# The state-space recurrence of a hybrid encoder on chunks of 8 steps instead of full-length scans

## The chip, the cores and the metric

One core of a Trainium2 chip runs the kernel. The metric is device time in microseconds (us) from the first to the last instruction of a run. The core has a matrix engine (TensorE, PE in the rows; its weight loads are PEld), a vector engine (VectorE, DVE), a scalar engine (ScalarE, ACT), a general engine (GpSimd, POOL) and a queue engine (SyncE, SP) that starts most transfers. Each engine takes its instructions in one fixed order and waits on semaphores for the others.

## What is computed

The reference is a trunk of two layers on 512 tokens of width 1024. Each layer has a mixer (three token mixers on the same input, gated and merged) and a mixture of 16 experts. The change touches the first token mixer, S5, a diagonal state-space model: 256 channels in 16 groups of 16, each group with 64 complex states. Cut to what matters, with the complex arithmetic as in the reference:

```python
lam_bar = jnp.exp(lam * dt)                       # (16 groups, 64 states), complex
b_bar = b * ((lam_bar - 1.0) / lam)[..., None]    # (16, 64, 16)
bu = einsum('blgc,gpc->blgp', uf, b_bar)          # input of every step
# state[t] = lam_bar * state[t-1] + bu[t], t = 0 .. 511
y = (einsum('blgp,gcp->blgc', real(states), c_re) - einsum('blgp,gcp->blgc', imag(states), c_im)
     + d_skip * uf)
y = gelu(y); y = y * sigmoid(y @ w_glu + b_glu)
```

The other two token mixers are stick-breaking attention (4 heads, a running sum along the keys) and chunkwise retention. Their sum, gated, goes through an output projection, a norm, the experts and another norm. All is held to single precision.

## The kernel before

**Matmuls and weights.** A large product in single precision is three passes with operands cut into a high and a low part (`mm3`, L343 to L345). A weight chunk comes by SyncE's queue (`load`, L317), ScalarE copies its high part `wh` (L337), and VectorE or GpSimd subtracts it from the raw values for the low part `wl` (L338), in halves of 128x1024. Which of the two engines does it in a mixer's chunk is a table, `LEND`. In the expert loops VectorE does nearly all of them.

**A layer.** The projection of the mixers runs in 22 chunks of 256 columns. Chunk 0 is the input of S5 (`s5_in`). Chunks 1 to 3 are queries, keys and values of the attention (`stick`): the first three chunks are made with tokens along the free axis (`pjf`, matmuls of 512 columns), the values with channels there (`pjt`, 256 columns). Ten units of attention follow, each a score product, two sigmoids on ScalarE, a scan on VectorE (L735), a product `take` (L737), transposes and a value product `pw` (L740 to L746). Then come retention (chunks 4 to 9), the gates (10 to 21), the output projection and the experts.

**S5 before.** `s5_params` makes, from the parameters, the table b (`bb`, split and spread into `small`), the decay `mag` and the table E of 128 powers of the unit rotation of each state, by doubling (L585 to L590). For layer 0 it runs on VectorE while the first chunks are projected, with half of the last doublings on GpSimd. For layer 1 it is a generator on GpSimd that takes a step in each expert loop of layer 0 from expert 4 on. `s5` then takes eight blocks of 128 states: six matmuls for real and imaginary inputs `bre` and `bim` over 512 tokens, six rotations by E (L642 to L647), two scans in four pieces of 128 with a carry fixed up between them (L658 to L662), six operations to rotate back (L664 to L669, one of them on GpSimd), and two fp32 matmuls `py` with the table c (L672, L673). Gelu and the gate `glu` (L689) end it.

**What sets the order.** A scheduler places the instructions of each engine in a fixed order, by the order of the program and by priorities. The parts of S5 are placed among the attention and the projections; `bre`, `bim` and `py` have high priority on TensorE.

Of the kernel before, what the change touches and what calls it, by code (L numbers as in the profile page):

```python
# [9 lines left out]
F32 = mybir.dt.float32  # L10
F32R = mybir.dt.float32r
# [8 lines left out]
P = 128  # L20
# [34 lines left out]
ST = SMALL["b"][0]  # L55


def shape_constants():
# [12 lines left out]
    misc[:, 40:48] = 2.0 ** np.arange(8)  # L71
# [20 lines left out]
def lay_out(a):  # L92
# [10 lines left out]
    for n in ("s5_d", "s5_b_glu", "ret_gn_g", "ln1_g", "ln1_b"):  # L103
# [3 lines left out]
    c = np.zeros((DEPTH, 2, 64, 2, 2, 4, 2, 16), np.float32)  # L107
    for ri, n in enumerate(("s5_c_re", "s5_c_im")):
        v = a[n].reshape(DEPTH, 2, 4, 2, 16, 64)
        for g in range(2):  # L110
            c[:, g, :, :, ri, :, g, :] = v[:, :, :, g].transpose(0, 4, 1, 2, 3)
    put("c", c)
# [4 lines left out]
    return dict(small=sm, router=rw)  # L117


class Kernel:  # L120
# [340 lines left out]
    def s5_loads(self, l, queue=None):  # L461
        self.s5b = self.sx[0].tile([P, ST + 2 * T], F32, tag="raw", name="small")
        sm = self.s5b[:, 0:SM]
        at = SMALL["c"][0]
        self.nc.scalar.dma_start(sm[:, 0:at], self.a["small"][l][:, 0:at])
        for i, j in ((ST, SM), (at, ST)):
            self.loaded = (queue or self.nc.scalar).dma_start(sm[:, i:j], self.a["small"][l][:, i:j]).ins
        return sm
# [5 lines left out]
    def s5_params(self, sp, sm, V, two):  # L474
        nc, mp = self.nc, self.keep
        bn = self.part(sm, "b").rearrange("p (r i c) -> p r i c", r=2, i=8)
        st2 = lambda nm, n, dt=F32, bufs=1: sp.tile([P, n], dt, tag=nm, name=nm, bufs=bufs)
        re, im, ldt = (self.part(sm, n) for n in ("s5_lambda_re", "s5_lambda_im", "s5_log_dt"))
        t = lambda nm, n=8: sp.tile([P, n], F32, name=nm, tag=nm)
        dt = self.poly_exp(sp, ldt, 8, V)  # L480
# [3 lines left out]
        mag = mp.tile([P, 8], F32, tag="mag", name="mag")  # L484
        V.tensor_copy(mag, self.poly_exp(sp, x, 8, V))
        N = 8 * LEVELS
        ang = sp.tile([P, LEVELS, 8], F32, name="ang")
        V.tensor_tensor(ang, th[:, None, :].to_broadcast([P, LEVELS, 8]),
                        self.misc[:, 40:40 + LEVELS, None].to_broadcast([P, LEVELS, 8]), OP.mult)
        af = ang.rearrange("p a b -> p (a b)")  # L490
# [25 lines left out]
        En = mp.tile([P, 2, LEVELS, 8], F32, tag="En", name="En")  # L516
        V.tensor_scalar(En[:, 0], cm.rearrange("p (a b) -> p a b", a=LEVELS), 1.0, None, OP.add)
        V.tensor_copy(En[:, 1], s.rearrange("p (a b) -> p a b", a=LEVELS))
        turn = mp.tile([P, 8, 2], F32, tag="turn", name="turn")
        V.tensor_copy(turn[:, :, 0], En[:, 1, 7])  # L520
        V.tensor_scalar(turn[:, :, 1], En[:, 1, 7], -1.0, None, OP.mult)
        lr, l1, li = t("lr"), t("l1"), t("li")
        V.tensor_tensor(lr, mag, cm[:, 0:8], OP.mult)
        V.tensor_tensor(lr, lr, mag, OP.add)
        V.tensor_scalar(l1, lr, -1.0, None, OP.add)
        V.tensor_tensor(li, mag, s[:, 0:8], OP.mult)
# [16 lines left out]
        v4 = lambda t, n=256: t[:, 0:n].rearrange("p (r i c) -> p r i c", r=2, i=8)  # L543
        zrb = zr[:, :, None].to_broadcast([P, 8, 16])
        zib = zi[:, :, None].to_broadcast([P, 8, 16])
        bb = v4(st2("bb", 256))
        q = st2("Et0", 256, bufs=2)[:, 0:128].rearrange("p (i c) -> p i c", i=8)
        V.tensor_tensor(bb[:, 0], bn[:, 0], zrb, OP.mult)
        V.tensor_tensor(q, bn[:, 1], zib, OP.mult)
        V.tensor_tensor(bb[:, 0], bb[:, 0], q, OP.subtract)  # L550
        V.tensor_tensor(bb[:, 1], bn[:, 0], zib, OP.mult)
        V.tensor_tensor(q, bn[:, 1], zrb, OP.mult)
        self.stt(V, bb[:, 1], bb[:, 1], -1.0, q, OP.mult, OP.subtract)
        bh = v4(st2("bh", 256, F32R))
        bl = bb
        yield
        nc.scalar.copy(bh, bb)
        yield
        V.tensor_tensor(bl, bb, bh.bitcast(F32), OP.subtract)
        for m in range(2):  # L560
            yield
            st = self.s5b[:, ST + m * T:ST + (m + 1) * T]
            sv = st.rearrange("p (k r q c) -> p k r q c", k=2, r=2, q=4)
            nc.gpsimd.memset(st, 0.0)
            for k, src in enumerate((bh.bitcast(F32), bl)):
                for g2 in range(2):
                    pp = slice(g2 * 64, g2 * 64 + 64)
                    V.tensor_copy(sv[pp, k, :, :, g2 * 16:g2 * 16 + 16], src[pp, :, 4 * m:4 * m + 4])
        yield
        e2 = self.sx[1].tile([P, 2 * 8 * P], F32, tag="raw", name="E")  # L570
        er, ei = (e2[:, i * 8 * P:(i + 1) * 8 * P].rearrange("p (a b) -> p a b", a=8) for i in range(2))
        nc.gpsimd.memset(er[:, :, 0:1], 1.0)
        nc.gpsimd.memset(ei[:, :, 0:1], 0.0)
        for j in range(LEVELS - 1):
            n = 2 ** j
            last = j >= LEVELS - (4 if two == 2 else 2)
            for hf, G in ((slice(0, 4), V), (slice(4, 8), nc.gpsimd)) if last else ((slice(0, 8), V),):
                w = hf.stop - hf.start
                cr = En[:, 0, j, hf, None].to_broadcast([P, w, n])
                ci = En[:, 1, j, hf, None].to_broadcast([P, w, n])  # L580
                a0, b0 = er[:, hf, 0:n], ei[:, hf, 0:n]
                a1, b1 = er[:, hf, n:2 * n], ei[:, hf, n:2 * n]
                t0 = st2(f"Et{hf.start * (two - 1)}", 256, bufs=2)[:, 0:w * n].rearrange("p (i n) -> p i n", i=w)
                t1 = st2(f"Et{hf.start * (two - 1)}", 256, bufs=2)[:, 0:w * n].rearrange("p (i n) -> p i n", i=w)
                G.tensor_tensor(a1, a0, cr, OP.mult)  # L585
                G.tensor_tensor(t0, b0, ci, OP.mult)
                G.tensor_tensor(b1, b0, cr, OP.mult)
                G.tensor_tensor(t1, a0, ci, OP.mult)
                G.tensor_tensor(a1, a1, t0, OP.subtract)
                G.tensor_tensor(b1, b1, t1, OP.add)  # L590
        E = [(er[:, 0:4], ei[:, 0:4]), (er[:, 4:8], ei[:, 4:8])]
        self.s5w = dict(mag=mag, En=En, turn=turn, E=E, sm=sm,
                        cT=self.part(sm, "c").rearrange("p (m r s) -> p m r s", m=2, r=2),
                        wg=self.part(sm, "w_glu").rearrange("p (k c) -> p k c", k=2))

    def s5_in(self, l, hh):
        nc = self.nc
        V = nc.vector
# [883 lines left out]
```

## Time and profile before

| what | value |
|---|---|
| three runs, median (lowest to highest) | 2286.53 us (2275.9 to 2291.71) |
| span of the profiled execution | 2285.9 us |
| time of that execution | 2285.9 us: nothing of note lies outside the span |
| TensorE busy | 2169.5 us |
| VectorE busy | 1738.9 us |
| ScalarE busy | 1228.1 us |
| GpSimd busy | 443.2 us |

Busy is the time in which an engine executes. The rest of the span it waits or issues. The share is an average over stages that differ: in the two mixers (about 20 to 300 us and 1157 to 1400 us) TensorE has gaps, in most of the expert loops it has none. The granted clock is the share of full speed (2.4 GHz) that TensorE gets; half of it is 1.2 GHz.

### The profile page before, as it was taken

Reading aid. Unit: us, or ns where it says so; the run is one execution under the profiler, and the core shown is the slowest. Engines: PE = TensorE matmul, PEld = TensorE weight load, DVE = VectorE, ACT = ScalarE, POOL = GpSimd, SP = SyncE. Lnnn points to the kernel's source line nnn. Section 1 sums busy time; section 2 is a strip of 40 time slices with the busy share of each in tenths; the row PEclk is TensorE's granted clock in tenths of the full one; section 3 lists DMA queues with packets and bytes.
Section 4 is the critical chain, followed back from the end, with each engine's and each line's share of the span. In section 5 each row is a group of like instructions: output and inputs, shape, how many; then the busy total and the mean of one; then the engine's idle time right before and its main releaser. Section 6 shows DMA issues by size and latency. Waiting matters only on the chain. (4 is left out here: it accounts for less than half of the span.)

```text
span 2285.9 us, 27438 instructions
## 1 busy us (share of the span) xinstructions
PE 2169.5 (95%) x10068; PEld 1586.7 (69%) x10069; DVE 1738.9 (76%) x2339; ACT 1228.1 (54%) x1526; POOL 443.2 (19%) x469
## 2 busy tenths in 40 slices
PE   6998999999999799999988989999899999999997
PEld 5656678877777577776655566888777777777765
DVE  8778753458988988887888875334689888888878
ACT  3231123336777577777732321232377777777774
POOL 4322051120049510000232210511300000000003
PEclk9898999999999899999999999999999999999999
DMA  5402245327989799997821021453289999999965
GB/s 184 152 32 57 65 152 187 113 79 286 339 313 350 266 360 345 338 376 278 344 92 56 19 70 65 166 180 120 79 318 336 358 345 359 349 351 359 345 256 212
DMA packets 180006, 517.22 MB, mean 226 GB/s; under 512 B 9808, under 2 KB 63696, under 8 KB 179856
## 3 DMA queue, kind: packets, MB, share of 16 engines
q1 hardware_dynamic: 167424, 475.91, 57.0%
q10 hardware_dynamic: 7312, 20.28, 2.5%
q0 software_dynamic: 5120, 19.14, 2.3%
q8 instruction: 82, 1.34, 0.2%
q14 instruction: 68, 0.56, 0.1%
HBM read 490.38 MB, written 22.81 MB: 225 GB/s over the span
## 5 line engine op out<-in xcount | busy, mean ns | idle before, releaser
L338 DVE TENSOR_TENSOR wl<-raw,wh 128x1024 fp32r<-128x1024 f32 x834 | 1025.3, 1247 | 275.3 <-ACT wh L337 258.1
L337 ACT CAST wh<-raw 128x1024 fp32r<-128x1024 f32 x872 | 906.1, 1050 | 489.2 <-PE e L345 210.7
L344 PE MATMUL e<-wl,hx 128*96 128x512 f32 x1024 | 406.6, 397 | 18.9 <-DVE wl L338 15.3
L345 PE MATMUL e<-wh,hx 128*96 128x512 f32 x1024 | 404.1, 395 | 0.0
L343 PE MATMUL e<-wh,hx 128*96 128x512 f32 x1024 | 391.9, 394 | 0.3 <-ACT wh L337 0.3
L344 PE MATMUL pjf<-hx,wh 128*128 128x512 f32 x608 | 246.3, 405 | 5.2 <-DVE hx L211 5.1
L343 PE MATMUL pjf<-hx,wh 128*128 128x512 f32 x608 | 247.7, 408 | 1.6 <-DVE v L210 1.6
L345 PE MATMUL pjf<-hx,wl 128*128 128x512 f32 x608 | 245.7, 404 | 0.0
L344 PEld LDWEIGHTS e<-wl,hx 128*96 128x96 f32 x1024 | 165.6, 162 | 87.2 <-DVE wl L338 14.1
L343 PEld LDWEIGHTS e<-wh,hx 128*96 128x96 f32 x1024 | 165.4, 162 | 67.7 <-ACT wh L337 0.7
L345 PEld LDWEIGHTS e<-wh,hx 128*96 128x96 f32 x1024 | 165.7, 162 | 65.6
L345 PE MATMUL e<-wh,gl 128*96 128x512 f32 x512 | 201.3, 393 | 0.0
L344 PE MATMUL e<-wl,gh 128*96 128x512 f32 x512 | 201.1, 393 | 0.2
L343 PE MATMUL e<-wh,gh 128*96 128x512 f32 x512 | 194.7, 393 | 0.0
L1335 POOL DMA_INDIRECT yg<-yd,pos x16 | 27.4, 1714 | 856.0 <-DMA raw<-in_moe_w_dram 843.1
L344 PEld LDWEIGHTS pjf<-hx,wh 128*128 128x128 f32 x608 | 117.1, 193 | 40.9 <-issue 9.4
L343 PEld LDWEIGHTS pjf<-hx,wh 128*128 128x128 f32 x608 | 117.1, 193 | 33.6 <-issue 7.6
L345 PEld LDWEIGHTS pjf<-hx,wl 128*128 128x128 f32 x608 | 117.0, 192 | 32.0 <-issue 7.7
L338 POOL TENSOR_TENSOR wl<-raw,wh 128x1024 fp32r<-128x1024 f32 x38 | 93.0, 2458 | 132.1 <-ACT wh L337 120.7
L344 PEld LDWEIGHTS e<-wl,gh 128*96 128x96 f32 x512 | 82.7, 161 | 35.6 <-DVE wl L338 1.4
L343 PEld LDWEIGHTS e<-wh,gh 128*96 128x96 f32 x512 | 82.5, 161 | 35.1
L345 PEld LDWEIGHTS e<-wh,gl 128*96 128x96 f32 x512 | 82.5, 161 | 34.4
(484 smaller groups left out, 3025.9 us busy)
## 6 DMA issues: line engine op xcount, KB each, us to landing
raw<-in_moe_w_dram SPq DMA_DIRECT2D x384, 1024.0 KB, 5.5
raw<-in_w_in_dram SPq DMA_DIRECT2D x44, 1024.0 KB, 5.1
yd<-y ACTq DMA_DIRECT2D x28, 384.0 KB, 4.2
raw<-in_w_out_dram SPq DMA_DIRECT2D x8, 1024.0 KB, 7.5
yd<-zr POOLq DMA_DIRECT2D x2, 2688.0 KB, 22.4
row<-hd POOLq DMA_DIRECT2D x8, 512.0 KB, 5.2
rawu<-in_w_up_c_dram SPq DMA_DIRECT2D x8, 512.0 KB, 3.4
tab<-in_ct_dram ACTq DMA_DIRECT2D x12, 256.0 KB, 3.3
```

Source lines behind the costliest of these rows:

```text
L337: self.cut = (nc.scalar.copy(hv, v).ins, (eng or nc.vector).tensor_tensor(lv, v, hv.bitcast(F32), OP.subtract).ins)
L338: (eng or nc.vector).tensor_tensor(lv, v, hv.bitcast(F32), OP.subtract).ins)
L343: mm(out, lh, rh, start=start, stop=False)
L344: mm(out, lh, rl, start=False, stop=False)
L345: mm(out, ll, rh, start=False, stop=stop)
L1335: nc.gpsimd.indirect_dma_start(out=yg[j], out_offset=None, in_=Y[:, :], in_offset=bass.IndirectOffsetOnAxis(ap=r["pos"][:, j, c:c + 1], ax ...
```

## The change

The sequence is cut into 64 chunks of 8 steps. Within a chunk nothing is scanned: a table T of the products c·lam^k·b for the lags 0 to 7 (a block-triangular matrix of 128x128 for each group, with d on the diagonal) gives the part of the output that comes from the same chunk, as one matmul per group (`lags`, L707). A second table `into` (b times powers of lam) gives what a chunk adds to the state at its end, as 64x64 matmuls `gr` and `gi` (L701). One scan over the 64 chunks (16 scans of 64 columns, L723), with rotations by a table E of 64 powers of lam^8 around it, gives the states at the chunk ends, and a table `cx` (c times powers of lam) adds their part to the output (L738). The input must stand as (step, channel) by chunk for that, so it is transposed twice (`ua`, `ub`), and the output twice back (`ya`, `yb`). The tables b, c and E are not made in one place any more: `s5_params` makes 13 angles per state instead of 8, the powers of lam, the scaled b and, on GpSimd in both layers, the 24 products of the table c; `s5_tables` makes E on GpSimd (36 operations), the `vb` tables on VectorE, the lag products on TensorE and the table T by seven transfers on SyncE's queue, all at the time of the mixer. The low parts `ul`, the `bTp` transposes, the carries between pieces and the 128-column scans are gone; the new matmuls are plain fp32.

```diff
+CHUNK = 8
+STEPS = T // CHUNK
+TURNS = (*range(1, CHUNK + 1), *(CHUNK * 2 ** i for i in range(1, 6)))
...
     def s5_params(self, sp, sm, V, two):
...
+        for h in range(4):
+            yield
...
+            for r, (x0, x1) in enumerate(((lam[0], lam[1]), (lam[2], lam[0]))):
+                o = cx[r][:, hs, 1:]
+                G.tensor_tensor(o, c[0], x0, OP.mult)
+                G.tensor_tensor(w, c[1], x1, OP.mult)
+                G.tensor_tensor(o, o, w, OP.subtract)
-        for j in range(LEVELS - 1):
...
-                G.tensor_tensor(a1, a0, cr, OP.mult)
...
+    def s5_tables(self):
...
+        for j in range(6):
...
+            G.tensor_tensor(a1, a0, cr, OP.mult)
+            G.tensor_tensor(t0, b0, ci, OP.mult)
+            G.tensor_tensor(b1, b0, cr, OP.mult)
+            G.tensor_tensor(t1, a0, ci, OP.mult)
+            G.tensor_tensor(a1, a1, t0, OP.subtract)
+            G.tensor_tensor(b1, b1, t1, OP.add)
...
+                V.tensor_tensor(o, b[0], lam[r], OP.mult)
+                V.tensor_tensor(x, b[1], lam[1 - r], OP.mult)
+                V.tensor_tensor(o, o, x, (OP.subtract, OP.add)[r])
...
+                    nc.tensor.transpose(ps[:, i * P:(i + 1) * P], full[:, i * P:(i + 1) * P], self.ident)
...
+        G.memset(tt, 0.0)
...
+                        nc.tensor.matmul(ps[:, i * P:(i + 1) * P], bb[gs, r, 4 * h + i],
+                                         cx[r][gs, 4 * h + i, 0:CHUNK].rearrange("p m c -> p (m c)"),
+                                         start=r == 0, stop=r == 1, skip_group_check=True)
...
+        for j in range(1, CHUNK):
+            t3 = tt.rearrange("p (g x) -> p g x", g=16)
+            nc.sync.dma_start(t3[j * 16:(j + 1) * 16, :, j * 16:], t3[0:16, :, 0:(CHUNK - j) * 16])
...
+    def s5(self, uf, ys):
...
+        for r, o in enumerate((gr, gi)):
+            for i in range(8):
+                for g in range(2):
+                    at = (i % 4) * P + g * 64
+                    nc.tensor.matmul(o[g * 64:g * 64 + 64, ks(i)], into[r][i // 4][:, at:at + 64], ug(i, g),
+                                     start=True, stop=True, skip_group_check=True)
...
+                nc.tensor.matmul(Y[g][:, ks(i)], tt[:, (2 * i + g) * P:(2 * i + g + 1) * P], ug(i, g),
+                                 start=i == 0, stop=False, skip_group_check=True)
...
+        V.tensor_tensor(e8(xr), e8(gr), er, OP.mult)
...
+                V.tensor_tensor_scan(o[:, ks(i)], mag[:, i:i + 1].to_broadcast([P, STEPS]), x[:, ks(i)], 0.0,
+                                     OP.mult, OP.add)
...
+                    nc.tensor.matmul(Y[g][:, ks(i)], cx[r][gs, i, 1:].rearrange("p m c -> p (m c)"),
+                                     S[r][gs, ks(i)], start=False, stop=i == 7 and r == 1, skip_group_check=True)
-                        self.mm3(o, bT[m][qs, 0, r], bT[m][qs, 1, r], us[m][0][qs], us[m][1][qs], True, True)
...
-                    V.tensor_tensor_scan(rr[:, sl], mg.to_broadcast([P, P]), xr[:, sl], i0, OP.mult, OP.add)
...
-                    nc.tensor.matmul(o, w["cT"][:, m, 0, q * 32:q * 32 + 32], sr, start=True, stop=False)
-                    nc.tensor.matmul(o, w["cT"][:, m, 1, q * 32:q * 32 + 32], si, start=False, stop=True)
```

How the orders move, at three places. First GpSimd in layer 0, from the second half of chunk 2's low part to those of chunk 3 (`wl`; E, Et: the rotation table, `zr` a block of zeros that is written out to memory). Before:

```order
L338 TENSOR_TENSOR wl<-raw,wh 128x1024
L564 MEMSET small 128x512
L338 TENSOR_TENSOR wl<-raw,wh 128x1024
L585 TENSOR_TENSOR E<-E,En 128x4x16
...
L590 TENSOR_TENSOR E<-E,Et_460 128x4x64
L415 MEMSET zr 128x512
L338 TENSOR_TENSOR wl<-raw,wh 128x1024
L418 DMA yd<-zr 96x14x512 x2
```

And after (`small`, `s5c`: the two halves of the table c with its powers, `cw` a scratch tile), the end of the c products:

```order
L579 TENSOR_TENSOR cw<-s5c 128x256
L618 TENSOR_TENSOR er<-er,s5c 128x8x2
L619 TENSOR_TENSOR Et<-ei,s5c 128x16
L620 TENSOR_TENSOR ei<-ei,s5c 128x8x2
L621 TENSOR_TENSOR Et<-er,s5c 128x16
L580 TENSOR_TENSOR s5c<-s5c,cw 128x2x128
L582 TENSOR_SCALAR s5c<-s5c 128x8x16
L415 MEMSET zr 128x512
L338 TENSOR_TENSOR wl<-raw,wh 128x1024
L418 DMA yd<-zr 96x14x512
L338 TENSOR_TENSOR wl<-raw,wh 128x1024
L418 DMA yd<-zr 96x14x512
```

Before, the first half of chunk 3 stands ahead of the doublings and the second behind them. Now both stand behind all 24 c products (L578 to L580), and the second behind a DMA issue too.

Second, GpSimd where layer 1 begins, from the last norm operations of layer 0 to the low parts of chunk 1. Before:

```order
L272 TENSOR_TENSOR ve<-ve,cs 128x1
L298 TENSOR_SCALAR nb<-mv,ve 128x1
L338 TENSOR_TENSOR wl<-raw,wh 128x1024 x2
L734 MEMSET left 128x1 x4
```

After:

```order
L272 TENSOR_TENSOR ve<-ve,cs 128x1
L298 TENSOR_SCALAR nb<-mv,ve 128x1
L593 MEMSET uf 128x32 x2
L609 MEMSET er 128x8
L610 MEMSET ei 128x8
L647 MEMSET T 128x2048
L618 TENSOR_TENSOR er<-er,s5c 128x8
...
L621 TENSOR_TENSOR Et<-er,s5c 128x256
L622 TENSOR_TENSOR er<-er,Et 128x8x32
L623 TENSOR_TENSOR ei<-ei,Et 128x8x32
L338 TENSOR_TENSOR wl<-raw,wh 128x1024 x2
```

The clearing of T and all 36 doublings of E now stand between the norm and the low parts of chunk 1.

Third, TensorE in layer 0 behind chunk 0. Before:

```order
L343 MATMUL pjf<-hx,wh 128x512
L344 MATMUL pjf<-hx,wh 128x512
L623 MATMUL bTp<-cs,small 128x128 x8
L345 MATMUL pjf<-hx,wl 128x512
L343 MATMUL pjf<-hx,wh 128x512
L344 MATMUL pjf<-hx,wh 128x512
L343 MATMUL bre<-uh,bT 128x512
L344 MATMUL bre<-ul,bT 128x512
```

After, at the same stretch, TensorE has `pjf` alone (71 in a row) and goes straight on to chunk 3:

```order
L343 MATMUL pjf<-hx,wh 128x512
L344 MATMUL pjf<-hx,wh 128x512
L345 MATMUL pjf<-hx,wl 128x512
L343 MATMUL pjt<-wh,hx 128x256
L344 MATMUL pjt<-wl,hx 128x256
L345 MATMUL pjt<-wh,hx 128x256
```

The S5 matmuls that stood among these projections are gone; the new ones come among the attention's units (`vT`, `lag`, `ua`, `ub`, `gr`, `gi`) and behind them (`y`, `ya`, `yb`).

## Rows read from the trace of the kernel before

**Rows 1.** Page section 1: busy us (share) xinstructions of each engine.

```profile
PE 2169.5 (95%) x10068; PEld 1586.7 (69%) x10069; DVE 1738.9 (76%) x2339; ACT 1228.1 (54%) x1526; POOL 443.2 (19%) x469
```

**Rows 2.** TensorE's waits, whole span: waiting line <- releaser: us, times, longest.

```profile
PE py L672 <- DVE sr L666: 23.4, 8, 6.2
```

**Rows 3.** Windows by stage: length, busy us by engine, granted clock, DMA share.

```profile
40.00:90.00 50.00, 44.45 (x211) 34.24 (x209) 36.84 (x109) 11.37 (x16) 25.30 (x29) 0.86 0.52 168
...
164.00:258.00 94.00, 82.44 (x393) 59.11 (x392) 77.35 (x141) 18.16 (x30) 18.14 (x10) 0.91 0.20 59
...
1172.00:1245.00 73.00, 62.45 (x263) 41.33 (x262) 62.24 (x105) 14.72 (x20) 22.44 (x11) 0.93 0.20 65
...
1305.00:1362.00 57.00, 48.10 (x273) 35.83 (x272) 47.92 (x71) 17.95 (x32) 14.73 (x8) 0.91 0.18 51
```

**Rows 4.** TensorE's waits in layer 0's mixer, 40 to 265 us.

```profile
PE py L672 <- DVE sr L666: 11.8, 4, 6.2
PE bre L343 <- DVE xi L644: 5.2, 2, 2.9
PE bTp L623 <- DVE small L568: 2.5, 1, 2.5
```

**Rows 5.** TensorE's waits in layer 1's mixer, 1150 to 1362 us.

```profile
PE py L672 <- DVE sr L666: 11.6, 4, 4.1
PE pw L740 <- DVE take L737: 10.1, 5, 4.5
...
PE py L673 <- DVE si L669: 1.9, 1, 1.9
```

**Rows 6.** TensorE's timeline: start, length, line, operation, count; a length contains overlap.

```profile
47.74 1.56 PE L623 MATMUL bTp<-cs,small 128*128 128x128 f32 x7
...
254.35 0.40 PE L343 MATMUL pjf<-hx,wh 128*128 128x512 f32 x1
254.58 1.02 PE L689 MATMUL glu<-gel,small 128*128 128x512 f32 x2
255.44 0.38 PE L807 MATMUL rA<-vc,rpA 128*128 128x128 f32 x2
255.66 0.39 PE L807 MATMUL rA<-vc,rpB 128*128 128x128 f32 x2
```

**Rows 7.** Weight loads by line, 40 to 265 us: busy us, mean ns.

```profile
L344 PEld LDWEIGHTS pjf<-hx,wh 128*128 128x128 f32 x107 | 21.7, 202 | 7.8 <-issue 4.0
```

**Rows 8.** Timelines of VectorE, TensorE and GpSimd in layer 0.

```profile
43.13 0.16 DVE L525 TENSOR_SCALAR l<-lr 128x8 f32<-128x8 f32 x1
...
44.74 0.39 PE L344 MATMUL pjf<-hx,wh 128*128 128x512 f32 x1
...
62.13 2.35 POOL L338 TENSOR_TENSOR wl<-raw,wh 128x1024 fp32r<-128x1024 f32 x1
```

**Rows 9.** Timelines of GpSimd and VectorE where layer 1 begins.

```profile
1164.45 5.18 POOL L338 TENSOR_TENSOR wl<-raw,wh 128x1024 fp32r<-128x1024 f32 x2 [10.37 <-ACT wh L337]
...
1165.65 4.54 DVE L211 TENSOR_TENSOR hx<-v,hx 128x512 fp32r<-128x512 f32 x2
```

**Rows 10.** Timelines of VectorE, GpSimd and TensorE, 767 to 783 us.

```profile
767.45 18.38 DVE L338 TENSOR_TENSOR wl<-raw,wh 128x1024 fp32r<-128x1024 f32 x4 [1.79 <-ACT wh L337]
...
780.60 0.73 POOL L590 TENSOR_TENSOR E<-E,Et 128x256 f32<-128x256 f32 x1
...
770.33 0.40 PE L343 MATMUL e<-wh,hx 128*96 128x512 f32 x1
782.47 0.74 PE L344 MATMUL e<-wl,hx 128*96 128x512 f32 x1 [11.75 <-DVE wl L338]
```

**Rows 11.** Timelines of VectorE and GpSimd in the same set-up, 753 to 774 us.

```profile
753.22 6.67 DVE L338 TENSOR_TENSOR wl<-raw,wh 128x1024 fp32r<-128x1024 f32 x5 [0.20 <-ACT wh L337]
...
764.41 0.21 POOL L586 TENSOR_TENSOR Et<-E,En 128x16 f32<-128x16 f32 x1
...
774.00 0.62 POOL L585 TENSOR_TENSOR E<-E,En 128x256 f32<-128x256 f32 x1
```

More of the change, by code (lines that the diff above doesn't have):

```diff
@@ L54 @@
     SM += _w
-ST = SMALL["b"][0]
 def shape_constants():
@@ L569, in s5_params @@
[L569 to L573, printed above, removed]
-        for j in range(LEVELS - 1):
[L575 to L584, printed above, removed]
-                G.tensor_tensor(a1, a0, cr, OP.mult)
[L586 to L590, printed above, removed]
@@ L615, in s5 @@
         w = self.s5w
-        E, En, mag = w["E"], w["En"], w["mag"]
-        bT = []
+        mag, cx = w["mag"], w["cx"]
+        er, ei, into, tt = self.s5_tables()
+        U = []
         for m in range(2):
-            ps = self.bank("b", "bTp")
-            with self.tc.high_priority():
-                for x in range(4):
-                    at = ST + m * T + x * P
-                    nc.tensor.transpose(ps[:, x * P:(x + 1) * P], self.s5b[:, at:at + P], self.ident)
-            t = mp.tile([P, T], F32R, tag="bT", name="bT", bufs=2)
-            nc.scalar.copy(t, ps)
-            bT.append(t.rearrange("p (k r s) -> p k r s", k=2, r=2))
@@ new lines, in s5 @@
+            ps = self.bank("b", "ub")
+            for x in range(8):
+                nc.tensor.transpose(ps[:, x * STEPS:(x + 1) * STEPS],
+                                    ut[x // 4][:, x % 4].rearrange("p j c -> p (j c)"), self.ident[0:64, 0:64])
+            u = self.t2("U")
+            nc.scalar.copy(u, ps)
+            U.append(u)
+        ks = lambda i: slice(i * STEPS, (i + 1) * STEPS)
+        ug = lambda i, g: U[i // 4][:, ks(2 * (i % 4) + g)]
+        gr, gi = self.bank("b", "gr"), self.bank("b", "gi")
@@ new lines, in s5 @@
+        lags(0)
+        e8 = lambda x: x.rearrange("p (i k) -> p i k", i=8)
+        xr, xi, t1, t2 = (self.t2(n) for n in ("xr", "xi", "t1", "t2"))
+        V.tensor_tensor(e8(xr), e8(gr), er, OP.mult)
+        V.tensor_tensor(e8(t1), e8(gi), ei, OP.mult)
+        V.tensor_tensor(e8(xi), e8(gi), er, OP.mult)
+        V.tensor_tensor(e8(t2), e8(gr), ei, OP.mult)
+        V.tensor_tensor(xr, xr, t1, OP.add)
+        V.tensor_tensor(xi, xi, t2, OP.subtract)
+        Y[1] = self.bank("b", "y1")
+        lags(1)
@@ new lines, in s5 @@
+        rr, ri = self.t2("rr"), self.t2("ri")
+        for i in range(8):
+            for o, x in ((rr, xr), (ri, xi)):
+                V.tensor_tensor_scan(o[:, ks(i)], mag[:, i:i + 1].to_broadcast([P, STEPS]), x[:, ks(i)], 0.0,
+                                     OP.mult, OP.add)
+        S = [self.t2("sr"), self.t2("si")]
+        tmp = [self.t2("t3"), self.t2("t4")]
+        end = (slice(None), slice(None), slice(0, STEPS - 1))
+        for r, (x0, x1, op) in enumerate(((rr, ri, OP.subtract), (ri, rr, OP.add))):
+            s8, q8 = e8(S[r]), e8(tmp[r])
+            nc.gpsimd.memset(s8[:, :, 0:1], 0.0)
+            V.tensor_tensor(s8[:, :, 1:], e8(x0)[end], er[end], OP.mult)
+            V.tensor_tensor(q8[:, :, 1:], e8(x1)[end], ei[end], OP.mult)
+            V.tensor_tensor(s8[:, :, 1:], s8[:, :, 1:], q8[:, :, 1:], op)
@@ new lines, in s5 @@
+        for g in range(2):
+            gs = slice(g * 64, g * 64 + 64)
+            for i in range(8):
+                for r in range(2):
+                    nc.tensor.matmul(Y[g][:, ks(i)], cx[r][gs, i, 1:].rearrange("p m c -> p (m c)"),
+                                     S[r][gs, ks(i)], start=False, stop=i == 7 and r == 1, skip_group_check=True)
+        act = []
+        for g in range(2):
+            f = self.wide("gelu")
+            nc.gpsimd.memset(f[:, T:], 0.0)
+            q2 = self.t2("sq")
+            nc.scalar.activation(q2, Y[g], AF.Square)
+            V.tensor_scalar(q2, q2, 0.044715, 1.0, OP.mult, OP.add)
+            V.tensor_tensor(q2, q2, Y[g], OP.mult)
+            nc.scalar.activation(q2, q2, AF.Tanh, scale=math.sqrt(2.0 / math.pi))
+            V.scalar_tensor_tensor(f[:, 0:T], q2, 1.0, Y[g], OP.add, OP.mult)
+            act.append(f)
```

269 lines of the change are left out of this document (148 added, 121 removed).

## The prediction

> **What bounds the kernel now.** I read the page first. TensorE is busy 95% of the span, VectorE 76%, GpSimd 19% [rows 1]. So time can come from three places only: TensorE's own work, the 116 us (2285.9 less 2169.5) in which it idles, and the stretches at a lower granted clock. The list of TensorE's waits names who makes it idle: `py` of the state-space mixer waits for VectorE's rotated states, 23.4 us in eight waits, a fifth of the idling [rows 2]. Half as much again is one single wait in an expert loop, 11.75 us [rows 10]. Next, the windows by stage: around the s5 work the granted clock is 0.86 to 0.93, and VectorE is busy for 77.35 of 94 us in one stretch and 47.92 of 57 in another [rows 3]. The waits of each mixer alone give the terms below [rows 4, 5]. The expert loops run with TensorE full, and nothing in them but the parameter set-up of layer 1 is touched.
>
> The profiled execution took 2285.9 us, the median of the three runs is 2286.53, so a sum against the one holds for the other. The runs spread over 15.8 us (0.7%); I call a change of less than 1% (23 us) no change.
>
> **TensorE's work.** Removed per layer: 48 `bre`/`bim` matmuls, which at the full clock follow each other by 0.23 us like `pjf` (254.35 to 254.58), 11.0 us; 32 `py` instructions (16 fp32 matmuls, two passes each) at 0.43 us as `glu` (two from 254.58 to 255.44), 13.8 us; 8 `bTp` transposes at 0.11, 0.9 us [rows 6]. Together 25.7 us. Added: 80 transposes (vT, ua, ub, ya, yb, 16 each) and 112 small fp32 matmuls in two passes (32 lag tables, 32 `gr`/`gi`, 16 in-chunk lags, 32 carries), 304 instructions. The nearest row is `rA`, 128 columns, two passes per 0.22 us, 0.11 each [rows 6]: 304 by 0.11 is 33.4 us. 160 of them have 64 columns; if those cost 0.08, between half of 0.11 and all of it, the sum is 28.6. The dear end is the weight load, which lasts about 0.20 us on this stretch where each instruction brings its own [rows 7]: 304 by 0.20 is 61 us. I take +4 us per layer, near the cheap end, because `rA` also loads new weights and keeps 0.11. **+8 us**, from +6 to +70.
>
> **VectorE's work.** In s5 some 200 operations per layer (25 for each of eight blocks: rotations, scans of 128 columns and their carries, rotations back) become 44: twelve for the input table and four for the skip, six rotations, sixteen scans of 64 columns, six rotations back. That empties most of the busy time in [rows 3], but it buys time only where TensorE waits for it, which is counted next; on its own it is nothing.
>
> **Layer 0's mixer.** TensorE's waits on `py` (11.8), `bre` (5.2) and `bTp` (2.5) have no instruction left to happen at: −19.5 us [rows 4]. What is late next is the GpSimd queue. In the changed order GpSimd runs the 24 power products of the c table (128x256 each) and the first doubling levels before the `wl` of chunk 3, the values of the attention. Before, that `wl` started at 62.13, long before it was needed [rows 8]. Twelve operations of 128x256 take 7.3 us (774.00 to 781.33), 0.61 each, the longest 0.73 [rows 10, 11]; the inputs are ready on VectorE at about 43 us [rows 8], a little later with 104 instead of 64 angles. So 45 + 24 by 0.61 to 0.73 + 3 for the small ones + 2.4 for `wl` ends at 65 to 68 us. TensorE, without bTp and bre, has 61 `pjf` left at 44.97, and is through them at 59. New wait 6 to 9, and one or two more since the second half of the chunk stands behind a DMA issue on that queue: I take 10. The chain behind the attention (rotations, scans, carries, gelu, two rounds of transposes) is covered by 37 `pjf` at 0.23 and 88 `pjt` of half the columns at half of that, 18.6 us of filler; I charge 3 for its transposes and 3 for attention waits that lose filler here (in layer 1, with less of it, `pw` waits 10.1 [rows 5]). **−3.5 us.**
>
> **Layer 1's mixer.** `py` 11.6 and 1.9 go, −13.5 [rows 5]. `pw` I leave. New: after the last norm operation GpSimd clears the table T (128x2048) and runs all 36 doubling operations of E in a row, at the pace of the same operations in the trace 11 us (the upper five of the six levels from about 764.41 to 774.00, and a small one) [rows 11]; only then come the two `wl` of chunk 1, 5.18 us [rows 9]. At that place VectorE makes the eight `hx` residuals on which the first matmuls wait, and the trace shows what GpSimd does to them: the last pair took 4.54 us beside a `wl` that had begun at 1164.45 [rows 9]. Ends: nothing held but `wl` late, 2 us; all residuals held through memset and E, 13. I take 8, near the middle, plus 3 for the transposes at the end. **−2.5 us.**
>
> **The set-up in the expert loop.** The 11.75 us wait is one event [rows 10]: GpSimd ran the doublings of E without a gap to 781.33, a VectorE subtract that asked at 767.45 finished, with three more, 18.38 us later, and TensorE stood still to 782.47. It goes, since E moves into the mixer. But the same place gets the 24 c products, 24 by 0.61 = 14.6 us, one behind the other in GpSimd's queue. If VectorE is shut out all that time, the wait returns: 14.6 less the 3.1 us that TensorE ran on, 11.5 [rows 10]. If the two take turns, as from 753 to 760, where five subtracts took 6.67 us while GpSimd made the b table [rows 11], it costs nothing. I take the middle, **−6 us**, from −11.75 to 0.
>
> The Trainium skill (SBUF — State Buffer, section "SBUF: two separate sides") says that the port pair VectorE shares with GpSimd is locked for one whole instruction. By that alone the subtract would have waited for one operation, under 0.75 us; the 18.38 us row speaks for a hold over a streak. By that page the set-up term would be −11.75 and the new wait of layer 1 at its lower end; the time that this gives is part of the first rival.
>
> **The clock.** Low grants cost at most length by missing share: layer 0 7.0 + 8.5, layer 1 5.1 + 5.1, together 25.7 us [rows 3]. It was low where TensorE had waited: `bTp`, after 2.5 us of idling, goes at 0.21 us instead of 0.11 [rows 4, 6]. The stretches 164 to 258 and 1305 to 1362 (13.6 us) lose nearly all their waits; of the other two, which get one longer wait for several short ones, I count a third. **−18 us**, from −4 to −25.
>
> Sum: 8 − 3.5 − 2.5 − 6 − 18 = −22, that is **2264 us**.
>
> **The rivals.**
> - *The cover holds everywhere*: the c products take turns with VectorE (−6 more), layer 1's E costs 2 instead of 8, chunk 3 is 4 us less late, the transposes and attention cost nothing more (−9), and the clock gives 3 more: another 28, 2236 us. For it: the s5 work of VectorE falls to a quarter in both mixers, so little is left there to be held up. Against: a GpSimd streak is placed ahead of needed work three times.
> - *The waits change hands*: GpSimd shuts VectorE out at all three places, +6 in the set-up, +5 in layer 1, +2 in layer 0, and the stops keep 8 of what the clock gives: 2285, no change. For it: [rows 9, 10]. What would decide is whether the subtract beside the c products lasts over 10 us. The Trainium skill (GPSIMD Engine Reference, section 4.1) advises two-input elementwise work on VectorE, GpSimd being about twice as slow; by that rule the two tables are on the wrong engine, and the trace agrees: a `wl` of 128x1024 takes 2.35 us on GpSimd [rows 8], and on VectorE five take 6.67, 1.33 each [rows 11].
> - *Slower: small matmuls run at their weight load.* The place is the 304 new instructions. At 0.19 instead of 0.11 each a layer pays 58 less 26, so 32 instead of 4: 2264 + 56 = 2320. It starts to be slower than before from 0.14 each (42.6 less 25.7 is 17, 13 more per layer than the 4, which eats the 22), and by over 1% from about 0.18. For it: weight loads of 0.20 us on this stretch, and 0.21 per instruction at the low clock (seven `bTp` in 1.56 us [rows 6]); a chain of dependent short work is where the clock was low. Against: `rA` at 0.11.
> - *That the change doesn't do what it says* is excluded: the orders show py, bre and the 128-column scans gone.
>
> **The chances.** Forecast 0.42 (own range 2250 to 2278), cover holds 0.22, waits change hands 0.20, slower 0.16. The limit of 1% is 2263: half of the forecast's case (0.21) and the second (0.22) lie below, so faster 0.43. Same: the other half and nine tenths of the third, 0.39. Slower 0.18: the fourth and the rest of the third. The range from 2230 to 2300 leaves out a small part of the second case and most of the fourth.
>
> **What the profile after would show.** No wait at `py` or `bre`; in the set-up, c products (L578 to L580) and beside them either subtracts of 1.3 us or one of over 10; in layer 0 a TensorE wait of 6 to 11 us at about 59 us at the first `pjt`, released by GpSimd's `wl`; in layer 1 `hx` subtracts of several us beside L618 to L623; between 164 us and the end of layer 0's s5 a granted clock near 1.00; the 32 carry matmuls (L738) 0.08 to 0.11 us apart per pass. The forecast falls if the carries come 0.19 apart, or if another engine's queue holds the attention's start beyond 90 us.

## The result, and the profile after

The changed kernel takes 2255.76 us (median of four runs, 2254.71 to 2257.38), against 2289.02 for the kernel before in the four runs beside it: a ratio of 0.9865, with a 95% interval of 0.9837 to 0.9893. The profiled execution spans 2253.0 us, 32.9 less than before. The forecast was 2264, 22 less.

The page's first section after, which answers to [rows 1]:

```profile
PE 2163.2 (96%) x10500; PEld 1620.2 (72%) x10501; DVE 1540.8 (68%) x1970; ACT 1247.2 (55%) x1580; POOL 479.9 (21%) x509
```

VectorE lost 198 us of work and TensorE 6; TensorE's idle time went from 116.4 to 89.8 us. The waits of TensorE over the whole span (waiting line <- releaser: us in total, times, longest), which answer to [rows 2, 4, 5]:

```profile
PE pw L826 <- DVE take L823: 22.3, 10, 18.5
...
PE pjf L345 <- POOL wl L338: 7.3, 1, 7.3
...
PE pjt L344 <- POOL wl L338: 3.2, 2, 2.4
```

`py`, `bre` and `bTp` are gone from the list. In their place stand one wait of 18.5 us at the first transpose `pw` of the attention, and one of 7.3 us for a weight residual that GpSimd makes.

Where the time came from is read at marks that both programs have: the output projection `opj` of layer 0, the transposes `tp` between the layers, and `opj` of layer 1. Per tile and operation the view gives the count, the shortest, median and longest duration in ns, and the first and last start. Before:

```profile
L343 PE MATMUL opj<-wh,hx x64: 393/398/482, 449.5 to 502.1; 128*128 128x512 f32 x64
...
L1446 PE MATMUL tp<-cs,yg x32: 270/273/329, 1151.6 to 1156.4; 128*128 128x128 f32 x32
...
L343 PE MATMUL opj<-wh,hx x64: 393/398/481, 1585.3 to 1637.9; 128*128 128x512 f32 x64
```

And after:

```profile
L343 PE MATMUL opj<-wh,hx x64: 394/399/484, 447.7 to 500.2; 128*128 128x512 f32 x64
...
L1532 PE MATMUL tp<-cs,yg x32: 271/273/329, 1140.8 to 1145.7; 128*128 128x128 f32 x32
...
L343 PE MATMUL opj<-wh,hx x64: 392/399/484, 1551.4 to 1603.9; 128*128 128x512 f32 x64
```

| stretch | before, us | after, us | difference |
|---|---|---|---|
| start to first `opj` of layer 0 | 449.5 | 447.7 | −1.8 |
| from there to `tp`: projection and experts of layer 0 | 702.1 | 693.1 | −9.0 |
| `tp` to first `opj` of layer 1: its mixer | 433.7 | 410.6 | −23.1 |
| from there to the end | 700.6 | 701.6 | +1.0 |

The two mixers run the same program on the same sizes, and one gained 23 us and the other 2. That is the question that the experiments go after, and the second is what the 9 us in the experts are.

**Layer 0.** The rows around the 18.5 us wait, from the timelines of GpSimd, ScalarE and TensorE (start, length, line, operation, then idle time before and its releaser):

```profile
62.89 1.20 POOL L418 DMA_DIRECT2D yd<-zr  x1
64.11 2.37 POOL L338 TENSOR_TENSOR wl<-raw,wh 128x1024 fp32r<-128x1024 f32 x1
66.42 0.94 POOL L418 DMA_DIRECT2D yd<-zr  x1
...
92.54 1.04 ACT L337 CAST wh<-raw 128x1024 fp32r<-128x1024 f32 x1 [19.39 <-DMA raw<-in_w_in_dram]
...
96.33 0.60 ACT L815 ACTIVATE keep<-z 128x512 f32<-128x512 f32 x1
...
100.77 0.69 PE L826 MATMUL pw<-cs,take 128*128 128x128 f32 x2 [18.53 <-DVE take L823]
```

The two transfers that clear the spill rows in memory (5.5 MB) leave GpSimd's queue at 62.89 and 66.42, the first between the two halves of chunk 3's low part and the second behind them. The load of the weights of chunk 5 (the recorded expectations call them those of chunk 4) shares the transfer engines with them. It needs the raw buffer that the second of these halves reads, so it is asked for at 66.51, 3.6 us behind the first transfer, and lands at 92.5. ScalarE's next instruction is the high part of these weights, so it stands still for 19.4 us, and the first sigmoids of the attention (`keep`) come only behind it at 96.33, although their scores `z` start at 78.2 us. TensorE runs out of filler and waits. The transfers are no part of the change, but their place ahead of the load is. In the kernel before, GpSimd issued both behind the two halves, at the moment at which the load was asked for. The rows of that kernel, then those of the changed one (the issue on each queue, and at the end of the `raw` lines with 1024.0 KB the us from issue to landing):

```profile
64.42 2.14 POOL L418 DMA_DIRECT2D yd<-zr  x2
64.51 0.37 SPq L323 DMA_DIRECT2D raw<-in_w_in_dram  x1
raw<-in_w_in_dram SPq DMA_DIRECT2D x1, 1024.0 KB, 6.5
...
66.51 0.37 SPq L323 DMA_DIRECT2D raw<-in_w_in_dram  x1
raw<-in_w_in_dram SPq DMA_DIRECT2D x1, 1024.0 KB, 25.9
```

The same load took 6.5 us before and 25.9 after. Before, ScalarE made the high part of these weights at 86.75, and what released it was TensorE and not the load.

**Layer 1.** The rows of GpSimd, VectorE and TensorE that answer to [rows 9]:

```profile
1163.34 0.71 POOL L623 TENSOR_TENSOR ei<-ei,Et 128x256 f32<-128x256 f32 x1
1164.01 4.66 POOL L338 TENSOR_TENSOR wl<-raw,wh 128x1024 fp32r<-128x1024 f32 x2
...
1155.05 1.63 DVE L211 TENSOR_TENSOR hx<-v,hx 128x512 fp32r<-128x512 f32 x2
...
1166.40 0.80 PE L345 MATMUL pjf<-hx,wl 128*128 128x512 f32 x1 [7.25 <-POOL wl L338]
```

The 36 doublings ran from 1147.83 to 1164.0, and VectorE's residuals `hx` beside them took 1.28 to 1.63 us a pair: neither engine kept the other out for long. What TensorE waited for was the `wl` behind the doublings.

**The set-up.** VectorE and GpSimd at the place of [rows 10]:

```profile
766.52 9.27 DVE L338 TENSOR_TENSOR wl<-raw,wh 128x1024 fp32r<-128x1024 f32 x6 [1.78 <-ACT wh L337]
...
769.85 1.60 POOL L579 TENSOR_TENSOR cw<-s5c 128x256 f32<-128x256 f32 x1
```

Six subtracts took 9.27 us, 1.55 each, and each c product of GpSimd waited for one of them. Nobody stood still, and TensorE had no wait.

**The clock.** Windows of 5 us (length, busy us by engine with counts, granted clock, DMA share, GB/s):

```profile
180.00:185.00 5.00, 5.00 (x49) 4.93 (x49) 1.25 (x1) 0.00 (x0) 3.60 (x3) 1.00 0.91 278
185.00:190.00 5.00, 5.00 (x34) 5.00 (x32) 2.41 (x4) 1.23 (x2) 0.00 (x0) 0.61 0.02 4
190.00:195.00 5.00, 5.00 (x24) 4.88 (x24) 3.59 (x7) 1.87 (x4) 0.00 (x0) 0.50 0.00 0
```

The full 5 us of each window are TensorE's busy time, and yet the grant is at its lower level from about 186 to 196 us. The carries (L738) go two passes per 0.22 us before it and per 0.43 us in it. The same 10 us are there in layer 1 at 1285 to 1295.

### The profile page after: what moved, and what is told of

Same layout as the page of the kernel before. It is cut to its first block, busy times and chain, and to the rows that moved or that the text cites. A ratio compares the mean times of both kernels' runs of the same rounds, so it can differ in the third digit from the quotient of the medians.

```text
span 2253.0 us, 28020 instructions
## 1 busy us (share of the span) xinstructions
PE 2163.2 (96%) x10500; PEld 1620.2 (72%) x10501; DVE 1540.8 (68%) x1970; ACT 1247.2 (55%) x1580; POOL 479.9 (21%) x509
## 5 line engine op out<-in xcount | busy, mean ns | idle before, releaser
L821 DVE TENSOR_TENSOR_SCAN left<-keep,cs 128x256 f32<-128x256 f32 (+3 forms) x32 | 27.1, 878 | 142.6 <-ACT keep L815 142.6
## 6 DMA issues: line engine op xcount, KB each, us to landing
raw<-in_moe_w_dram SPq DMA_DIRECT2D x384, 1024.0 KB, 5.7
raw<-in_w_in_dram SPq DMA_DIRECT2D x44, 1024.0 KB, 5.2
raw<-in_w_out_dram SPq DMA_DIRECT2D x8, 1024.0 KB, 7.4
```

The costliest lines, as they stand in the source:

```text
L821: V.tensor_tensor_scan(lf[:, 0:n][:, ::-1], keep[:, at:at + n][:, ::-1], self.zero.to_broadcast([P, n]), 1.0, OP.mult, OP.add)
```

## The experiments

Each ran beside the kernel before, three rounds or more; ratios are to that kernel.

**1. The zeros written late.** The two transfers become 14 pieces, one behind each sum of the merge.

```diff
-                            for h in range(2):
-                                self.nc.gpsimd.dma_start(spill[:, :, h * T:(h + 1) * T],
...
+                    self.zeros = [lambda i=i: self.nc.gpsimd.dma_start(
+                        spill[:, i], zr[0:CAP, None, :].to_broadcast([CAP, D // P, P])) for i in range(SPILL)]
...
+                        added = nc.gpsimd.tensor_tensor(mg[m], mg[m], sg, OP.add).ins
+                        if self.zeros:
+                            with self.tc.issue_after(added):
+                                self.zeros.pop(0)()
```

> The changed kernel with the zeros for the spill rows (5.5 MB in two transfers in the middle of layer 0's projections) written in 14 pieces during the merge instead. Theory 1: in layer 0 the gain of the change was lost because these transfers hold up the weights of chunk 4, whose high part stands ahead of the first sigmoid in ScalarE's queue, so that TensorE idles 18.5 us at the first pw; then the wait goes and the time falls by 14 to 19 us, to about 2239. Rival: layer 0 is bound by TensorE's work and its filler, and the wait only moves; then 2252 to 2258.

Measured 2247.59 us (2247.42 to 2249.66), 0.9844 [0.9801, 0.9887]: some 8 us less than the changed kernel by the medians, half of what I expected. Its waits in layer 0, 20 to 320 us:

```profile
PE pjt L345 <- POOL wl L339: 10.3, 2, 5.8
PE pw L826 <- DVE take L823: 3.9, 5, 2.1
```

The 18.5 us wait is gone, so the zeros were its cause. But without the transfers in its queue GpSimd ran 34 of the 36 doublings ahead of chunk 3's second `wl` instead of 10, and TensorE waits for the low parts of chunk 3 twice, 10.3 us. The first score came at 85.3 instead of 78.2 us.

**2. The same in the kernel before.** The diff is that of 1.

> The kernel before with the zeros written late in the same way. Theory 1: before, the projections of layer 0 last until 88 us, when the zeros have landed, so the same edit gives 0 to 5 us, 2284 to 2289. Rival, that the zeros cost both kernels the same and the change has nothing to do with it: 14 us or more, 2275 or less.

2291.74 us, 1.0023 [1.0003, 1.0044], so nothing was gained and perhaps 0.2% lost. The edit also moved the first score from 88.0 to 103.2 and layer 0's `opj` from 449.5 to 456.1, as the order of the projections shifted, so the run alone does not show that the zeros cost the kernel before nothing. Its trace does: the load landed in 6.5 us, and ScalarE did not wait for it. The loss is one that the change brought about.

**3. Layer 1's E on VectorE, in the kernel before.**

```diff
-            for hf, G in ((slice(0, 4), V), (slice(4, 8), nc.gpsimd)) if last else ((slice(0, 8), V),):
+            for hf, G in ((slice(0, 4), nc.vector), (slice(4, 8), nc.gpsimd if two == 2 else nc.vector)) if last else ((slice(0, 8), nc.vector),):
```

> The kernel before with the doublings of layer 1's table E made by VectorE instead of GpSimd in the expert loop, nothing else. Theory 1: the 11.75 us wait in the set-up comes from the GpSimd streak alone and about 10 us of the gain of the change is this and not the chunks: 2276 to 2280. Rival: VectorE is so full there that its own doublings delay the subtracts as much, or the hold moves to the next streak: 2284 to 2290.

2284.44 us, 0.9986 [0.9964, 1.0008]: no change that can be told, and the expectation missed. The 11.75 us wait is gone, but VectorE runs the doublings in one block, in a window (columns as above) with 82 of its instructions where it has 41 to 45 elsewhere:

```profile
900.00:950.00 50.00, 50.00 (x242) 36.80 (x241) 41.34 (x41) 37.93 (x46) 0.00 (x0) 1.00 0.97 346
950.00:1000.00 50.00, 41.31 (x179) 29.25 (x179) 42.93 (x82) 29.28 (x36) 0.00 (x0) 0.87 0.74 272
```

There TensorE waits 4.9 and 3.7 us and loses clock. So this edit did not isolate the wait, and the next does.

**4. The same, a level per expert step.**

```diff
+            if two == 1 and j > 2:
+                yield
```

> The kernel before with the doublings of layer 1's E on VectorE, the upper levels one per expert step instead of in one block. Theory 1: the set-up's wait can be had without the chunks; in pieces of at most 2.4 us the doublings hide under VectorE's slack and the time is 2275 to 2281, 10 to 13 less than before. Rival: the expert loops of layer 0 are paced by something else than that wait, and its removal gives at most 3 us.

2276.17 us, 0.9939 [0.9922, 0.9956]. The marks:

```profile
L343 PE MATMUL opj<-wh,hx x64: 393/398/482, 445.7 to 498.3; 128*128 128x512 f32 x64
...
L1448 PE MATMUL tp<-cs,yg x32: 271/273/328, 1138.9 to 1143.7; 128*128 128x128 f32 x32
```

From `opj` to `tp` it is 693.2 us, against 702.1 before and 693.1 in the changed kernel. So the 9 us of the experts come from moving E alone and could be had without the chunks. The ratio gives 14 us for the whole kernel; where the other 5 come from, one profile does not show.

**5. Idle GpSimd work in the set-up of the changed kernel.** Behind the c products come 36 operations of 128x128 in the pattern of the doublings (`dw<-x*cr`, `r<-y*ci`, ...), whose values nobody uses.

```diff
+        if two == 1:
+            yield
...
+            for j in range(6):
...
+                G.tensor_tensor(w1, x0, cr, OP.mult)
+                G.tensor_tensor(t0, y0, ci, OP.mult)
...
+                G.tensor_tensor(y0, w2, t1, OP.add)
```

> The changed kernel with 36 idle GpSimd operations of 128x128 added behind layer 1's set-up in the expert loop, in the pattern of the doublings of the kernel before (values not used). Theory 1: such a streak shuts VectorE's subtracts out for its whole length and a wait of 8 to 12 us at an expert matmul comes back: 2264 to 2270. Rival, since the 24 c products took turns with VectorE: these do too, no wait over 2 us, 2253 to 2259.

2267.8 us, 0.9902 [0.9865, 0.994]: the time of theory 1, and not by its mechanism. In the expert loops the added operations took turns with the subtracts, as the rival said, and no wait came. The 12 us are in layer 1's mixer, where the code is unchanged (`tp` to `opj` takes 422.5 us instead of 410.6), and a part of them at its start (VectorE, GpSimd, TensorE):

```profile
1149.17 12.08 DVE L211 TENSOR_TENSOR hx<-v,hx 128x512 fp32r<-128x512 f32 x2
...
1154.78 0.73 POOL L639 TENSOR_TENSOR ei<-ei,Et 128x256 f32<-128x256 f32 x1
1155.45 4.65 POOL L338 TENSOR_TENSOR wl<-raw,wh 128x1024 fp32r<-128x1024 f32 x2
...
1160.70 0.79 PE L344 MATMUL pjf<-hx,wh 128*128 128x512 f32 x1 [10.60 <-DVE hx L211]
```

Here a pair of `hx`, asked for at 1149.17 while the doublings were already running, finished 12.08 us later, when GpSimd's whole streak and the two `wl` behind it were done. In the changed kernel itself the same pairs took 1.28 to 1.63 us, beside doublings that began some 4 us later against `tp`. So a GpSimd streak can shut VectorE out. The number and the kind of its operations do not decide it, for they were the same, while the order of the instructions around them was not; what decides it stays open.

The hold is not the whole 12 us either. TensorE's wait is 10.6 us instead of 7.3, and the first score of layer 1 starts 4.3 us later. Some 5 us more are lost in the attention, where the granted clock is 0.50 from about 1241 to 1259 and 1.00 in the changed kernel, and the rest around the lags and carries, where the fall lasts longer. That the hold brought these on is not shown.

**6. The E of both mixers on VectorE, in the changed kernel.**

```diff
-            G.tensor_tensor(a1, a0, cr, OP.mult)
+            V.tensor_tensor(a1, a0, cr, OP.mult)
```

(and so for the other five operations of a level).

> The changed kernel with the 36 doublings of E in each mixer on VectorE instead of GpSimd. Theory 1: in layer 1 the low parts of chunk 1 then start some 16 us earlier on GpSimd and the 7.3 us wait of TensorE on them goes, 5 to 9 us less, 2247 to 2251; layer 0 is unchanged. Rival: the doublings on VectorE come ahead of the hx residuals of layer 1, or the wait is followed by another of the same length: 2254 to 2262.

2250.28 us (2245.91 to 2261.86), 0.987 [0.9818, 0.9922]. The interval holds the changed kernel's ratio, so the time alone tells nothing; the trace does: `tp` to `opj` of layer 1 fell from 410.6 to 403.1 us and the 7.3 us wait is gone, as expected, while layer 0 kept a wait of 19.3 us.

**7. gr, gi and the lags twice.**

```diff
-        for r, o in enumerate((gr, gi)):
+        for r, o in enumerate((gr, gi, gr, gi)):
+            r = r % 2
...
-            for i in range(8):
+            for i in list(range(8)) * 2:
```

> The changed kernel with the gr/gi and the in-chunk lag matmuls issued twice (96 more instructions per layer, the second pass overwrites the first with the same values). Theory 1: small matmuls are on TensorE's path at what the trace shows for them, 2.5 us for 64 gr/gi instructions and 3.7 for 32 lags: 12 to 16 us more, 2267 to 2272. Rival, that they run in the shadow of the scans: at most 4 us more. Third, that they cost their weight load of 0.19 us each or pull the clock down: 25 us or more.

2267.85 us, 0.9904 [0.9867, 0.9941], 12 us more by the medians. The instructions:

```profile
164.32 1.10 PE L702 MATMUL gr<-U,V 128*64 128x64 f32 x32
165.26 1.10 PE L702 MATMUL gi<-U,V 128*64 128x64 f32 x32
...
178.29 7.25 PE L708 MATMUL y<-U,T 128*128 128x64 f32 x64
```

32 instructions of `gr` go from 164.32 to 165.26, 0.03 each, and a lag takes 0.11. Per layer 64 by 0.03 and 32 by 0.11 make 5.5 us, twice that 11; by the marks layer 0 up to `opj` took 6.3 us more and layer 1's mixer 5.4. The added work is on TensorE's path at its traced pace, and the rival by which small matmuls cost their weight load is out.

**8. No carries.** The 32 carry matmuls per layer (L738) are left out, and with them the part of the output that comes from earlier chunks.

```diff
-            for i in range(8):
-                for r in range(2):
-                    nc.tensor.matmul(Y[g][:, ks(i)], cx[r][gs, i, 1:].rearrange("p m c -> p (m c)"),
-                                     S[r][gs, ks(i)], start=False, stop=i == 7 and r == 1, skip_group_check=True)
+            V.scalar_tensor_tensor(S[0][:, 0:8], S[1][:, 0:8], 0.0, Y[g][:, 0:8], OP.mult, OP.add)
```

(the added line, on VectorE, reads a few columns of the states.)

> The changed kernel without the 32 carry matmuls per layer (the part of the output that comes from earlier chunks is left out). Theory 1: TensorE's clock falls to half for some 10 us in each layer because the block of 32 lag and 64 carry instructions of 64 columns fills the engine's time but not its array; without the carries the fall goes and the gain is the instructions, 64 by 0.11, and 5 us of clock, per layer: 24 us, 2229 to 2235. Rival: the fall comes from something else behind the scans (gelu, transposes) and stays: the gain is 14 us, 2240 to 2244.

2238.46 us (2235.94 to 2238.65), 0.9771 [0.9738, 0.9804], 17 us less by the medians, between the two numbers. The windows bear on the question (columns as above):

```profile
180.00:185.00 5.00, 5.00 (x45) 5.00 (x44) 3.48 (x8) 2.26 (x5) 3.50 (x3) 1.00 0.97 311
185.00:190.00 5.00, 5.00 (x46) 4.67 (x44) 4.69 (x9) 2.39 (x7) 0.00 (x0) 1.00 0.04 12
190.00:195.00 5.00, 5.00 (x32) 3.47 (x31) 1.32 (x3) 3.08 (x8) 0.00 (x0) 1.00 0.01 3
```

The grant is 1.00 here, and so it is in layer 1 where the carries stood. In all seven traces of the changed kernel and its variants that have the carries it falls to 0.50 there in both layers, so this fall comes with them. They are not the only work that can have one. Without them a new low stretch stands in the attention of layer 1, with TensorE busy in it, over work that the changed kernel ran at 1.00:

```profile
1230.00:1235.00 5.00, 5.00 (x16) 2.28 (x14) 0.88 (x3) 1.03 (x3) 0.13 (x2) 0.50 0.01 3
```

Two by 64 by 0.11 is 14 us of the 17 (by the medians) to 21 (by the ratios). Between the first lag and `glu` of layer 1 10.7 us went, 7.0 for the carries and 3.7 for the clock, and the new stretch gave some of that back. What a fall hangs on beyond the presence of this work stays open.

**9. All three edits: zeros late, E and layer 0's c products on VectorE.**

```diff
-        G = nc.gpsimd
+        G = nc.vector if two == 2 else nc.gpsimd
```

(in the set-up, beside the edits of 1 and 6.)

> The changed kernel with three edits: zeros written late, the doublings of E in both mixers on VectorE, and layer 0's 24 c products on VectorE, so that GpSimd has only the low parts there. Theory 1: what layer 0 loses is order on GpSimd and on the transfer queues; with all three the first score matmul of layer 0 comes at about 72 us (78 and 85 in the kernels with the edits apart) and the time is 2230 to 2240. Rival: each wait removed is followed by another, the edits don't add up beyond the better of the two alone: 2245 to 2250.

2228.82 us (2222.59 to 2239.33), 0.9747 [0.9704, 0.979], the fastest kernel of this study, 27 us below the changed one by the medians. Its runs spread over 17 us, and the profiled one is the fastest of them. Its waits in layer 0, and its first scores:

```profile
PE pw L826 <- DVE take L823: 3.8, 5, 2.1
PE pjf L344 <- DVE v L211: 3.8, 1, 3.8
...
L809 PE MATMUL z<-kb,qb x32: 272/482/694, 71.7 to 124.8; 64*128 64x256 f32 x8, 64*128 64x128 f32 x8, 64*128 64x384 f32 x8, 64*128 64x512 f32 x8
```

The longest wait for an engine in this view is now for the first norm (`v`), the scores come at 71.7 us, and layer 0's `opj` starts at 424.4 instead of 447.7: layer 0 gained 25.1 us over the kernel before, as layer 1 had.

**10. As 9, with the zeros where they were.** The diff of 1 is undone:

```diff
-                        if self.zeros:
-                            with self.tc.issue_after(added):
-                                self.zeros.pop(0)()
...
+                            for h in range(2):
+                                self.nc.gpsimd.dma_start(spill[:, :, h * T:(h + 1) * T],
```

> The changed kernel with E in both mixers and layer 0's c products on VectorE, the zeros where they were. Theory 1: the zeros still stand between chunk 3 and the weights of chunk 4, and since the attention could start at 72 us, TensorE's wait for its first product is as long as before or longer (18 to 24 us), so this is 2246 to 2252 and the late zeros are worth some 20 us in the kernel with all three edits. Rival: with GpSimd free the zeros leave earlier and are out of the way, 2235 or less, and the three edits don't need each other.

2239.46 us (2229.05 to 2246.08), 0.9788 [0.9751, 0.9825]. Both numbers missed, but the rival's mechanism is what happened: the first score comes at 71.7 us too, and there is no wait at `pw` beyond 2.2. ScalarE had the weights in time:

```profile
47.19 10.49 POOL L338 TENSOR_TENSOR wl<-raw,wh 128x1024 fp32r<-128x1024 f32 x2 [6.02 <-ACT wh L337]
57.70 0.37 SPq L323 DMA_DIRECT2D raw<-in_w_in_dram  x1
58.45 2.15 POOL L418 DMA_DIRECT2D yd<-zr  x2 [0.31 <-POOL zr L415]
...
70.42 1.05 ACT L337 CAST wh<-raw 128x1024 fp32r<-128x1024 f32 x1 [3.78 <-PE pjt L345]
...
74.65 0.60 ACT L815 ACTIVATE keep<-z 128x512 f32<-128x512 f32 x1
```

With GpSimd free, the low parts of chunk 3 were done by 57.6 us, the weights of chunk 5 were asked for at 57.70, ahead of the zeros at 58.45, landed in 5.8 us, and the collision did not happen, though the scores came earlier still. What held layer 0 back was therefore the order on GpSimd, and the zeros were its price. The late zeros add 6.5 us by the spans (2227.3 and 2220.8); the medians say 10.6, with intervals that overlap.

## Why the prediction held, and where it was off

The direction was right and the time lies in the range, a third more gain than forecast. Step by step:

- **TensorE's work, +8: right.** The new instructions go at 0.03 to 0.11 us, the cheap end (experiment 7). At these paces the added sum per layer is some 27 us against the 25.7 removed, so +2 or +3 for both layers.
- **py, bre, bTp: right.** All three waits are gone, 11.8, 5.2 and 2.5 us in layer 0 [rows 4] and 13.5 in layer 1 [rows 5].
- **The late wl of chunk 3 in layer 0: right in kind, too dear.** I had 10 us; TensorE waited 3.2, because GpSimd began at 42.9 instead of 45 and finished the c products at 60.1, and TensorE came to chunk 3 at 60.3 instead of 59.
- **What is late next in layer 0: wrong.** This is the step that failed. I saw that the second half of chunk 3 stands behind a DMA issue, charged one or two us of GpSimd's queue for it, and put what the transfer itself does at nothing. I followed the `wl` and not the load behind it, which now stood behind 5.5 MB of zeros (25.9 us to land instead of 6.5), nor ScalarE's queue behind that load. Against my 3 us for the attention TensorE lost 18.5. By its own sign the forecast fell here: another engine's queue held the attention's start beyond 90 us, with the first sigmoid at 96.33.
- **Layer 1's start, 8: right by its sum, wrong by its mechanism.** 7.3 us came from the late `wl` and next to nothing from a hold. Experiment 5 shows that the hold could have come, with a wait of 10.6 us, by the same code in another order.
- **pw in layer 1, "I leave": wrong.** It fell from 10.1 to 2.1 us, 8 us that I had not counted. VectorE, busy for 62.24 of 73 us there before [rows 3], is busy for 22.10 of 50 us from 1215 to 1265.
- **The set-up, −6: too small.** The c products took turns with the subtracts throughout; the stretch gave 9.0, and experiment 4 gives the same.
- **The clock, −18: mis-sized.** From the windows the length by missing share in the mixers (0 to 300 us and 250 us of layer 1) went from 22 and 15 us to 22 and 10: 5 us of gain. The low stretches before did lose their waits, but new ones came in: in layer 0 behind the waits of 2.4 and 18.5 us, in layer 1 behind the one of 7.3, and in both beside the carries, where TensorE was busy all the time (experiment 8). The forecast tied the low clock to waits alone.

What the errors came to is read from TensorE's busy time in each stretch (length, then PE busy and the other engines, granted clock, DMA share, GB/s): up to layer 0's `opj` and layer 1's mixer, before and then after.

```profile
0.00:449.50 449.50, 410.56 (x1819) 302.14 (x1821) 292.56 (x573) 130.18 (x196) 127.13 (x132) 0.95 0.35 117
1151.60:1585.30 433.70, 402.00 (x1819) 295.77 (x1818) 268.08 (x431) 124.27 (x190) 104.29 (x87) 0.96 0.27 93
...
0.00:447.70 447.70, 405.85 (x2035) 317.89 (x2037) 199.04 (x363) 139.44 (x223) 136.81 (x172) 0.95 0.38 118
1140.80:1551.40 410.60, 396.55 (x2036) 311.57 (x2035) 171.41 (x272) 133.10 (x218) 111.44 (x124) 0.98 0.31 99
```

TensorE's busy time in the two mixers, work and clock together, fell by 10.2 us, and the forecast has 8 − 18 = −10 for it. How that splits is not shown: +2 or +3 for the work and −5 for the clock do not add up to it. TensorE's idle time rose by 2.9 us in layer 0's mixer (38.9 to 41.9) where the forecast has −3.5, and fell by 17.6 in layer 1's (31.7 to 14.1) where it has −2.5. So that the time came so near is in part luck: layer 0 lost in the attention some 6 us more than forecast, layer 1 came in 15 us better, and the set-up 3. Of the hold that the Trainium skill (SBUF — State Buffer, section "SBUF: two separate sides") puts at one instruction, the runs show both: 1.55 us per subtract beside the c products, which agrees, and 12.08 us beside the doublings in experiment 5, which does not.

## What to carry to other kernels

When a change moves an order, list which bulk transfer now leaves ahead of a load that someone needs, and who stands in a queue behind that load; here a write of 5.5 MB issued 3.6 us ahead of a 1 MB load made it land in 25.9 us instead of 6.5, and TensorE lost 18.5. An engine that becomes free is worth what the bound engine waits for it, stage by stage, and small work that is moved to a third engine is priced by what stands behind it in that queue. When several edits move waits between the same queues, try them together: by the medians zeros and E alone gave some 8 and 5 us (the 5 lies within that run's spread), the three together 27.

## What the runs showed of the hardware that was not expected

- TensorE's grant fell to 0.50 for about 10 us in each layer beside 96 narrow instructions of lags and carries, while it was busy 5.00 of each 5 us; without the carries it stayed at 1.00 there. A stretch of the attention, busy too, ran at 1.00 in one kernel and at 0.50 in another.
- Two fp32 passes of 64 columns with 64 weight columns (`gr`) go every 0.06 us, 0.03 each, though `LDWEIGHTS` of other tiles lasts 0.20.
- The same streak of GpSimd operations let VectorE's pairs through in 1.28 to 1.63 us in one kernel and held one for 12.08 us in another.
- A 1 MB load landed in 6.5 us when it was asked for in the same moment as a write of 5.5 MB on another queue, in 5.8 us when 0.75 us ahead of it, and in 25.9 us when 3.6 us behind its first half.
